# Eight pairs of the down projection's right half by seven products, with four small moves beside it

## The chip, the core and the metric

The kernel runs on one core of a Trainium2 chip. TensorE (PE in the profile) multiplies matrices into eight accumulator banks; VectorE (DVE), ScalarE (ACT) and GpSimd (POOL) do the elementwise work; SyncE (SP) and POOL issue the DMA transfers used here. The metric is the device time of one execution, in microseconds (us).

## The reference

Two layers, each a mixer (differential attention with eight heads beside a gated short convolution) and an MLP with squared ReLU, on 256 tokens of width 2048, all in float32:

```python
for l in range(DEPTH):
    h = _rmsnorm(x, attn_norm_g[l])
    proj = h @ w_in[l]
    ...
    x = x + jnp.concatenate([attn, conv.astype(attn.dtype)], axis=-1) @ w_out[l]

    hm = _rmsnorm(x, mlp_norm_g[l]) @ w_up[l]
    x = x + jnp.square(jax.nn.relu(hm)) @ w_down[l]
```

Here w_up is 2048 x 8192 and w_down 8192 x 2048, so the hidden activation of the MLP is 256 x 8192.

## The kernel before

Every product of float32 values is made of three matmuls. An operand is split into a high part (a copy to the float32r type on ScalarE) and a low part (value minus high part, on VectorE), and high x high, high x low and low x high are added up in an accumulator bank. So each weight tile costs one copy and one subtraction before TensorE can use it. TensorE's order is the program's own order, written out by hand. The other engines' instructions are ordered by a scheduler when the program is built, except those marked `late`, which keep their place.

Weights come as a list of jobs (`Weights`, line 283): a job loads a raw tile and splits it; `take` (line 353) hands out the next one and starts the jobs of the next three. There are three buffers for split halves. Small work beside the matmuls (transposes, attention, norms) is written as generators. `Background.tick` (line 74) is called between groups of matmuls; a generator that yields n goes on n ticks later.

The MLP (`mlp`, line 779) runs in two stages. The hidden activation is made in 32 pairs of 128 columns. While pair i comes out of the up projection (`up_part`, line 911), pair i - 2 goes into the left half of the down projection (columns 0 to 1023). Pairs 0 to 29 do this by seven products instead of eight: `square` (line 934) forms the sums S1 to S4 of the activation's quarters, `quarters` (line 818) forms sums of the weight's quarters (b1, b2, t13, t24), and `product` (line 958) is called seven times, with three matmuls of 512 columns each. Pairs 30 and 31 follow by ordinary products, 24 matmuls a pair (line 1042). The tile `h`, in which a pair's activation is formed, has one buffer. Each pair's squared activation is stored to DRAM (`hid`, line 943) from POOL's queue.

The second stage is the right half (columns 1024 to 2047, line 1069). It reads `hid` back in blocks of two pairs over SP's queue (`block`, line 1015), splits them again, and runs 16 blocks by two groups of 512 columns, all by ordinary products (`dn`, line 1081). Its pool opens only when the pool of the weight quarters has closed (line 1012). Then the next layer's norm begins: `norm.chunk` (line 439) transposes one quarter of x through two banks (`bank`, three buffers) and splits it.

In the mixer, `attention` (line 575) is started for each half of the heads three ticks after that half's v is done, and its last transposes come 12 ticks after its last unit. `Norm.factors` (line 484) broadcasts the ratio of the norm's two row factors with one small matmul (`rbc`, line 503), five ticks after the factors.

Of the kernel before, what the change touches and what calls it, by code (L numbers as in the profile page):

```python
# [15 lines left out]
P = 128  # L16
DEPTH = 2
D = 2048
S = 256
# [16 lines left out]
NB2 = DFF // (KG * P)  # L36

# [64 lines left out]
def trunk(ctx: ExitStack, tc: tile.TileContext, x, w_in, w_out, conv_w, q_norm_g, k_norm_g,  # L102
# [326 lines left out]
    class Norm:  # L429
# [54 lines left out]
        def factors(self):  # L484
# [8 lines left out]
            if self.which:  # L493
# [7 lines left out]
                yield 5  # L501
# [73 lines left out]
    def attention(l, qT, kT, kL, v, h0, dst, bias, tmp):  # L575
# [8 lines left out]
        def unit(i):  # L584
# [78 lines left out]
            yield 12  # L663
# [42 lines left out]
    def mixer(l, norm, loads):  # L706

        with ExitStack() as scope:
# [28 lines left out]
            for half in range(2):  # L737
# [15 lines left out]
                work.start(attention(l, qT, kT, kL, v, h0, cat[half], bias, tmp), 3)  # L753
# [25 lines left out]
    def mlp(l, mnorm, last):  # L779
# [3 lines left out]
        with ExitStack() as scope:  # L783
            upool = scope.enter_context(tc.tile_pool(name="upool", bufs=3))
            fpool = scope.enter_context(tc.tile_pool(name="fpool", bufs=2))
            dpool = scope.enter_context(tc.tile_pool(name="dpool", bufs=2))
            first = scope.enter_context(ExitStack())
            spool = first.enter_context(tc.tile_pool(name="spool", bufs=1))
# [22 lines left out]
            def load_rows(i, col):  # L811
                raw = dpool.tile([P, 2, 2 * CH], F32, tag="draw", name="draw")
# [5 lines left out]
            def quarters(i):  # L818


                keep = late if i == 0 else lambda ins: None
# [8 lines left out]
                def plain():  # L830
                    raw = forms["raw"] = load_rows(i, 0).rearrange("p k (n c) -> p k n c", n=2)
# [19 lines left out]
                if i == 0:  # L851
# [6 lines left out]
            def rows(i, k, box):  # L858
                def make():
                    if k == 0:  # L860
                        box.append(load_rows(i, 0))
# [22 lines left out]

            order = [(b - n, n) for b in range(NB2 + 1) for n in range(2) if 0 <= b - n < NB2]

# [12 lines left out]
            for b, n in order:  # L899
                box = []  # L900
                four(b, n, 0, box)
                four(b, n, 2, box)


            hid = [dram.tile([P, KG * S], F32, name=f"hid{l}{b}") for b in range(NB2)]
# [28 lines left out]
            def square(i, h):  # L934
# [8 lines left out]
                nc.gpsimd.dma_start(hid[i // 2][:, i % 2 * 2 * S:(i % 2 + 1) * 2 * S], u)  # L943
                n = 4
                if i < NP - LAG:
# [4 lines left out]
                    nc.vector.tensor_sub(h[:, S4], h[:, A12], h[:, S2])  # L950
                f = fpool.tile([P, 2, 8, P], F32R, tag="f", name="f")
# [6 lines left out]
            def product(n, j, a, b, stop=False):  # L958

                for m, (pa, pw) in enumerate(TERMS):  # L960
                    nc.tensor.matmul(prods[n], fs[j][:, pa, a], b[pw], start=(j == 0 and m == 0),  # L961
                                     stop=(stop and m == 2))

            fs = {}
            for i in range(NP):
# [14 lines left out]
                for c in range(2):  # L980
# [15 lines left out]
                    if j >= 0 and c == 0:  # L996
                        b11, b21, b22 = weights.take()
                        t1, t3 = weights.take()
                        product(1, j, A11, b11, end)
                        product(2, j, A12, b21)  # L1000
                        product(3, j, S4, b22)
                        product(5, j, S1, t1, end)
                        work.tick()
                    elif j >= 0:
                        t2, t4 = weights.take()
                        product(7, j, S3, t3, end)
                        product(6, j, S2, t2, end)
                        product(4, j, A22, t4)
                        work.tick()


            first.close()
            gpool = scope.enter_context(tc.tile_pool(name="gpool", bufs=3))

            def block(b):

                back = gpool.tile([P, KG * S], F32, tag="back", name="back", bufs=2)
                nc.sync.dma_start(back, hid[b])
                f = gpool.tile([P, 2, KG, S], F32R, tag="g", name="g")
                flat = f.rearrange("p a k s -> p a (k s)")  # L1020
                nc.scalar.activation(flat[:, 0], back, AF.Copy)
                nc.vector.tensor_sub(flat[:, 1], back, flat[:, 0].bitcast(F32))
                return f

            blocks = {0: block(0)}
# [5 lines left out]
            x11, x21, x12, x22 = (xs[n][:, t] for n in range(2) for t in range(NT))  # L1031
            e1, e2, e3, e4 = wide("e1"), wide("e2"), wide("e3"), wide("e4")
            nc.scalar.activation(e1, prods[1], AF.Copy, scale=mnorm.scale)
            onto(e2, prods[6], e1)
            onto(e4, prods[5], e2)
            onto(x22, prods[5], x22)
            onto(e3, prods[7], e2)
            for dst, v in ((x11, e1), (x12, e4), (x21, e3), (x22, e3)):
                nc.gpsimd.tensor_tensor(dst, dst, v, op=ALU.add)

            prods[8] = ps.tile([P, CH], F32, tag="av", name=f"pr{l}8", bufs=1)
            for j in range(NP - LAG, NP):
                for k in range(2):
                    b = weights.take()
                    for n, t, p in ((0, 0, 2), (0, 1, 4), (1, 0, 3), (1, 1, 8)):
                        for m, (pa, pw) in enumerate(TERMS):
                            nc.tensor.matmul(
                                prods[p], fs[j][:, pa, 2 * k + t], b[pw][:, n],
                                start=(p == 8 and j == NP - LAG and k == 0 and m == 0),
                                stop=(j == NP - 1 and k == 1 and m == 2))  # L1050
                    work.tick()
            for dst, p in ((x11, 2), (x21, 4), (x12, 3), (x22, 8)):
                onto(dst, prods[p], dst)
# [9 lines left out]
            else:  # L1063
# [77 lines left out]
```

## Time and profile before

| | |
|---|---|
| median of three runs | 2167.16 us |
| lowest and highest | 2166.77 and 2170.96 us |
| the profiled execution | 2167.59 us |
| its span, first to last instruction | 2165.8 us |
| mean granted TensorE clock | 0.999 |
| DMA, mean over the span | 206 GB/s |

How to read the lines below. A group's line names the source line, the engine, the operation, the output and inputs, their shapes and the count; then its busy time in us and the mean in ns; then the engine's idle time ahead of it and what ended that. A line of the chain is a start, a length and an instruction, for the sequence that ended last. In the table of waits the three numbers are the total in us, how often, and the longest. PEld is TensorE's weight load, which overlaps its matmuls.

### The profile page before, as it was taken

The numbers are of one execution on the slowest core, as the hardware profiler recorded it, in microseconds if no ns is written. First come the engines' busy times: TensorE is split into PE (matmuls) and PEld (weight loads), VectorE is DVE, ScalarE is ACT, GpSimd is POOL, SyncE is SP. The second block draws the span as 40 slices with busy tenths as digits, with TensorE's granted clock in tenths as the row PEclk, the third lists the DMA queues.
The fourth block names the chain that finished last, engine by engine and source line by source line (L and its number), as shares of the span: only waits on it lengthen the run. The fifth ranks groups of instructions, "written<-read, shape, count | busy, mean of one in ns | idle before, by whom it ended". The sixth has DMA issues, their size and how long they took to land.

```text
span 2165.8 us, 28903 instructions
## 1 busy us (share of the span) xinstructions
PE 2146.9 (99%) x10988; PEld 1828.7 (84%) x10988; DVE 1612.4 (74%) x2197; ACT 1294.1 (60%) x1743; POOL 135.3 (6%) x178
## 2 busy tenths in 40 slices
PE   9999999999999999999999999999999999999999
PEld 8888888888888888888888888888888888888887
DVE  6777655698888888855566776557988888887554
ACT  6666445566666666654456654446666666665443
POOL 3111100000000000100011111000000000001000
PEclk9999999999999999999999999999999999999999
DMA  8556666576666666577566566656766666666774
GB/s 271 179 162 210 189 188 186 170 235 216 214 211 214 218 216 215 196 257 242 174 213 176 160 215 190 185 165 204 233 211 213 216 219 215 211 213 211 246 242 147
DMA packets 292507, 446.62 MB, mean 206 GB/s; under 512 B 10419, under 2 KB 191237, under 8 KB 292368
## 3 DMA queue, kind: packets, MB, share of 16 engines
q1 hardware_dynamic: 285664, 423.66, 62.4%
q0 software_dynamic: 6656, 21.10, 2.5%
q8 instruction: 86, 1.41, 0.3%
q14 instruction: 53, 0.43, 0.1%
q10 hardware_dynamic: 48, 0.02, 0.0%
HBM read 425.84 MB, written 18.90 MB: 205 GB/s over the span
## 4 chain that ended last, share of the span: by engine, by line
PE 92%; DVE 3%; DMA 2%; ACT 2%; issue 1%; SPq 0%; DVEq 0%; ACTq 0%
PE upc L921 29%; PE dn L1081 16%; PE pr L961 13%; PE o L382 8%; PE gb L404 4%; PE k L382 4%; PE v L382 4%; PE ci L404 4%; PE q L382 4%; PE gc L404 3%; DMA raw<-in_w_in_dram 1%; PE upw L921 1%; PE sc L594 1%; DMA back<-hid 1%; DVE ulo L807 1%
## 5 line engine op out<-in xcount | busy, mean ns | idle before, releaser
L299 DVE TENSOR_TENSOR wlo<-raw,whi 128x1024 fp32r<-128x1024 f32 x382 | 468.9, 1229 | 364.1 <-ACT whi L298 363.3
L298 ACT ACTIVATE whi<-raw 128x1024 fp32r<-128x1024 f32 x382 | 404.6, 1060 | 448.9 <-PE dn L1081 167.8
L921 PE MATMUL upc<-nT,uhi 128*128 128x512 f32 x1920 | 477.5, 391 | 0.0
L806 ACT ACTIVATE uhi<-uraw 128x1024 fp32r<-128x1024 f32 x256 | 271.1, 1060 | 286.5 <-PE upc L921 253.4
L921 PEld LDWEIGHTS upc<-nT,uhi 128*128 128x128 f32 x1920 | 352.7, 188 | 68.2
L807 DVE TENSOR_TENSOR ulo<-uraw,uhi 128x1024 fp32r<-128x1024 f32 x256 | 312.8, 1222 | 113.5 <-ACT uhi L806 111.0
L1081 PE MATMUL dn<-whi,g 128*128 128x512 f32 x1024 | 316.3, 389 | 0.0
L921 PEld LDWEIGHTS upc<-nT,ulo 128*128 128x128 f32 x1920 | 261.9, 190 | 18.7
L921 PE MATMUL upc<-nT,ulo 128*128 128x256 f32 x1920 | 267.7, 282 | 0.0
L1081 PEld LDWEIGHTS dn<-whi,g 128*128 128x128 f32 x1024 | 192.2, 188 | 39.6
L1081 PE MATMUL dn<-wlo,g 128*128 128x512 f32 x512 | 199.7, 390 | 1.1 <-DVE wlo L299 0.9
L382 PE MATMUL o<-whi,cat 128*128 128x512 f32 x512 | 159.5, 390 | 0.0
L1081 PEld LDWEIGHTS dn<-wlo,g 128*128 128x128 f32 x512 | 96.1, 188 | 22.6 <-DVE wlo L299 2.8
L382 PEld LDWEIGHTS o<-whi,cat 128*128 128x128 f32 x512 | 96.2, 188 | 19.7
L382 PE MATMUL o<-wlo,cat 128*128 128x512 f32 x256 | 99.6, 389 | 0.0
L943 POOL DMA_DIRECT2D hid<-h x64 | 34.9, 545 | 946.0 <-ACT h L942 912.0
L961 PE MATMUL pr<-t13h,f 128*128 128x512 f32 x240 | 93.8, 391 | 0.0
L382 PE MATMUL k<-whi,nT 128*128 128x512 f32 x256 | 84.3, 396 | 0.0
L961 PE MATMUL pr<-t24h,f 128*128 128x512 f32 x240 | 84.0, 391 | 0.0
L961 PE MATMUL pr<-b2h,f 128*128 128x512 f32 x240 | 84.0, 391 | 0.0
L382 PE MATMUL v<-whi,nT 128*128 128x512 f32 x256 | 83.2, 395 | 0.0
L382 PE MATMUL q<-whi,nT 128*128 128x512 f32 x256 | 82.8, 394 | 0.0
(349 smaller groups left out, 3477.2 us busy)
## 6 DMA issues: line engine op xcount, KB each, us to landing
uraw<-in_w_up_dram SPq DMA_DIRECT2D x128, 1024.0 KB, 5.9
raw<-in_w_in_dram SPq DMA_DIRECT2D x191, 512.0 KB, 4.0
draw<-in_w_down_dram SPq DMA_DIRECT2D x64, 1024.0 KB, 5.1
raw<-in_w_down_dram SPq DMA_DIRECT2D x64, 1024.0 KB, 5.4
raw<-in_w_out_dram SPq DMA_DIRECT2D x64, 512.0 KB, 3.6
hid<-h POOLq DMA_DIRECT2D x64, 256.0 KB, 4.4
back<-hid SPq DMA_DIRECT2D x32, 512.0 KB, 3.4
rev<-by_dist_d POOLq DMA_DIRECT2D x4, 1024.0 KB, 10.0
```

The lines of the kernel that those rows point to most:

```text
L298: pair = (nc.scalar.activation(hi, raw, AF.Copy), nc.vector.tensor_sub(lo, raw, hi.bitcast(F32)))
L299: nc.vector.tensor_sub(lo, raw, hi.bitcast(F32)))
L382: nc.tensor.matmul(acc[:, t], a.ap[:, pa, k % KG, t * P:(t + 1) * P], (hi, lo)[pw][:, j], start=(k == 0 and n == 0), stop=(k == nk - 1 and ...
L404: nc.tensor.matmul(acc[:, f, 0] if part else acc[:, f], wt[:, k % 4, fs], a.ap[:, 0, k % KG] if part else a.ap[:, :, k % KG], start=(part ...
L594: nc.tensor.matmul(sc[m][:, OFF[t]:OFF[t] + W], qT[:, m, i, t * P:(t + 1) * P], k[:, m, i, :W], start=(k is kT), stop=(k is kL))
L806: nc.scalar.activation(hi, src, AF.Copy)
L807: nc.vector.tensor_sub(lo, src, hi.bitcast(F32))
L921: nc.tensor.matmul(acc[:, 0] if part else acc, wt[:, k], a.ap[:, 0, k % KG] if part else a.ap[:, :, k % KG], start=(part == 0 and kh == 0 ...
L943: nc.gpsimd.dma_start(hid[i // 2][:, i % 2 * 2 * S:(i % 2 + 1) * 2 * S], u)
L961: nc.tensor.matmul(prods[n], fs[j][:, pa, a], b[pw], start=(j == 0 and m == 0), stop=(stop and m == 2))
L1081: nc.tensor.matmul(acc[:, t], f[:, pa, k, t * P:(t + 1) * P], (hi, lo)[pw][:, k % 2], start=(b == 0 and k == 0 and m == 0), stop=(b == NB2 ...
```

## The change

- In the right half, pairs 2, 5, 8, 11, 14, 17, 20 and 23 go by seven products. The other pairs of 0 to 23 go by ordinary products, pair by pair; pairs 24 to 29 go in blocks as before. Pairs 30 and 31 are not stored and read back, but used first, from the tiles that the left half left in SBUF.
- A seven pair stores its activation with the sums (eight tiles of 128 columns instead of four), after the sums. Read-backs are issued from POOL's queue, into existing tiles, and their split goes to the pool that held the norm's transposed activation.
- The raw weight tiles of the MLP get a fourth buffer, and the lower quarters (b2) a second. The pool of the quarters stays open.
- The second half's attention starts six ticks after its v instead of three, and its last transposes come 18 ticks after the last unit instead of 12. The ratio's broadcast comes eight ticks after the factors instead of five.
- Chunks 0 and 1 of the next norm start 8 and 16 ticks after the right half's seven products are added to x (before: 12 and 24 ticks after the left half).

```diff
+SEVEN = (2, 5, 8, 11, 14, 17, 20, 23)
+BLK = 12
...
-                yield 5
+                yield 8
                 tp = bank("rbc")
...
-            yield 12
+            yield 12 if pace == 1 else 18
...
-                work.start(attention(l, qT, kT, kL, v, h0, cat[half], bias, tmp), 3)
+                work.start(attention(l, qT, kT, kL, v, h0, cat[half], bias, tmp,
+                                     1 + half), 3 * (1 + half))
...
-            upool = scope.enter_context(tc.tile_pool(name="upool", bufs=3))
+            upool = scope.enter_context(tc.tile_pool(name="upool", bufs=4))
...
-                    h2, l2 = parts(raw[:, 1], "b2", 1)
+                    h2, l2 = parts(raw[:, 1], "b2", 2)
...
-            order = [(b - n, n) for b in range(NB2 + 1) for n in range(2) if 0 <= b - n < NB2]
+            order = [(b - n, n) for b in range(BLK, NB2) for n in range(2)
+                     if BLK <= b - n < NB2 - 1]
...
+            blocks_of([(NB2 - 1, 0), (NB2 - 1, 1)])
+            for i in range(2 * BLK):
+                if i in SEVEN:
+                    weights.jobs += quarters(i, 2 * CH)
+                    continue
                 box = []
-                four(b, n, 0, box)
-                four(b, n, 2, box)
+                for k in range(2):
+                    rows(i, k, box, 2 * CH, upool, "uraw")
+            blocks_of(order)
...
-                nc.gpsimd.dma_start(hid[i // 2][:, i % 2 * 2 * S:(i % 2 + 1) * 2 * S], u)
+                if i not in SEVEN and i < NP - LAG:
+                    nc.gpsimd.dma_start(hid[i // 2][:, i % 2 * 2 * S:(i % 2 + 1) * 2 * S], u)
...
+                if i in SEVEN:
+                    nc.gpsimd.dma_start(hid7[i], h.rearrange("p a c -> p (a c)"))
...
+            def read_back(src, pool, tag, n):
+
+                back = (fpool.tile([P, 8, P], F32, tag="h", name="back", bufs=1) if n == 8 else
+                        nat.tile([P, 4, P], F32, tag="wide", name="back"))
+                nc.gpsimd.dma_start(back.rearrange("p a c -> p (a c)"), src)
+                f = pool.tile([P, 2, 8, P], F32R, tag=tag, name="fb")
+                nc.scalar.activation(f[:, 0, :n], back, AF.Copy)
+                nc.vector.tensor_sub(f[:, 1, :n], back, f[:, 0, :n].bitcast(F32))
+                return f
...
+            fs = {30: fs[30], 31: fs[31], 0: pair(0)}
+            for n in range(2):
+                columns(lambda k, pa, t: fs[NP - LAG + k // 2][:, pa, k % 2 * 2 + t], n, start=True)
+            for i in range(2 * BLK):
+                if i + 1 < 2 * BLK:
+                    fs[i + 1] = pair(i + 1)
+                else:
+                    blocks = {BLK: block(BLK)}
+                if i not in SEVEN:
+                    ordinary(fs[i])
+                    continue
...
+                for n, a, b in ((1, A11, b11), (2, A12, b21), (3, S4, b22), (5, S1, t1),
+                                (7, S3, t3), (6, S2, t2), (4, A22, t4)):
+                    own = n in (1, 5, 6, 7)
+                    product(n, fs[i], a, b, start and own, end and own)
+                    if n == 5:
+                        work.tick()
+                work.tick()
+            seven_onto(2, nc.vector)
+            if not last:
+                work.start(norm.chunk(0, 2), 8)
+                work.start(norm.chunk(1, 2), 16)
...
+            for b, n in order:
+                if n == 0 and b + 1 < NB2 - 1:
+                    blocks[b + 1] = block(b + 1)
+                columns(lambda k, pa, t, f=blocks[b]: f[:, pa, 2 * k + t], n,
+                        stop=(b == NB2 - 2))
```

`ordinary` and `columns` are the old loops of lines 1042 and 1076 made into functions; `seven_onto` is the old code of lines 1031 to 1039 (its additions to x on POOL for the left half, on VectorE for the right).

More of the change, by code (lines that the diff above doesn't have):

```diff
@@ L573, in qk_norm, with attention @@
             yield 1
-    def attention(l, qT, kT, kL, v, h0, dst, bias, tmp):
+    def attention(l, qT, kT, kL, v, h0, dst, bias, tmp, pace):
         parts = dst.open()
@@ L1062, in mlp, with columns @@
                 store(1)
-            else:
-                work.start(norm.chunk(0, 2), 12)
-                work.start(norm.chunk(1, 2), 24)
-            accs = {}
-            for b, n in order:
-                if n == 0:
-                    if b + 1 < NB2:
-                        blocks[b + 1] = block(b + 1)
-                if b == 0:
-                    accs[n] = mm.tile([P, NT, CH], F32, tag="mm2", name=f"dn{l}{n}")
-                f, acc = blocks[b], accs[n]
+            accs = [mm.tile([P, NT, CH], F32, tag="mm2", name=f"dn{l}{n}") for n in range(2)]
+            prods[2], prods[4] = accs[0][:, 0], accs[0][:, 1]
+            prods[3], prods[8] = accs[1][:, 0], accs[1][:, 1]
+            def columns(f, n, start=False, stop=False):
                 for kp in range(KG // 2):
```

123 lines of the change are left out of this document (68 added, 55 removed).

## Prediction

> **What bounds the kernel now.** I read the busy table of the page first, then the table of what TensorE waited for, then the chain of waits in order of time, then busy times by stage.
>
> ```profile
> PE 2146.9 (99%) x10988; PEld 1828.7 (84%) x10988; DVE 1612.4 (74%) x2197; ACT 1294.1 (60%) x1743; POOL 135.3 (6%) x178
> ```
> ```profile
> PE sc L594 <- ACT kT L545: 4.1, 2, 2.0
> PE pr L961 <- DVE f L953: 2.3, 3, 1.0
> PE atp L667 <- DVE an L658: 1.6, 2, 1.0
> PE pr L1047 <- DVE wlo L299: 1.6, 2, 0.8
> PE up L921 <- ACT ev L931: 1.4, 2, 0.7
> PE rbc L503 <- DVE diag L500: 1.1, 2, 0.5
> PE warm L156 <- DVE mhalf L148: 1.0, 1, 1.0
> PE dn L1081 <- DVE wlo L299: 0.9, 2, 0.5
> ```
> ```profile
> 165.62 2.79 PE gc L404 x16
> ...
> 604.03 5.56 PE upc L921 x32
> ...
> 948.66 130.58 PE dn L1081 x576
> ```
>
> TensorE is busy nearly everywhere, and its named waits sum to 14 us, each a fraction of a microsecond to 2 us. A matmul of 512 columns in the down projection takes 130.58/576 = 0.2267 us of the chain (its listed 0.39 us overlaps the next one). So the time is the number of matmuls, plus the waits. Every matmul taken away counts in full unless an engine that feeds TensorE falls behind.
>
> ```profile
> core 0: us, PE busy (x) PEld busy (x) DVE busy (x) ACT busy (x) POOL busy (x), PEclk, DMA share, GB/s
> ...
> 450.00:890.00 440.00, 438.70 (x2340) 378.62 (x2339) 389.71 (x525) 295.91 (x360) 15.14 (x28) 1.00 0.69 217
> ...
> 932.00:1089.00 157.00, 157.00 (x702) 130.25 (x701) 90.18 (x84) 77.11 (x85) 2.31 (x3) 1.00 0.64 208
> ```
>
> The first row is the up projection with the left half of the down projection by seven products: VectorE is busy 89% of TensorE's time, and TensorE hardly waits (2.3 us at L961 in both layers). The second is the right half, by ordinary products: VectorE at 57%. So the right half has VectorE time left, and seven products take VectorE time for fewer matmuls.
>
> **The change part by part.**
>
> *Matmuls.* A pair by ordinary products is 24 matmuls, by seven products 7 x 3 = 21. Eight pairs in each of two layers: 48 matmuls fewer, 48 x 0.2267 = **-10.9 us**. Nothing else changes the count.
>
> *Feeding the right half.* Three pairs (two ordinary, one by seven) are 69 matmuls, 15.64 us of TensorE.
>
> ```profile
> L299 DVE TENSOR_TENSOR wlo<-raw,whi 128x1024 fp32r<-128x1024 f32 x66 | 80.8, 1225 | 72.1 <-ACT whi L298 72.1
> ...
> L827 DVE TENSOR_TENSOR t13l<-t,t13h 128x1024 fp32r<-128x1024 f32 x28 | 34.3, 1226 | 0.8 <-ACT t13h L826 0.3
> L953 DVE TENSOR_TENSOR f<-h,f 128x1024 fp32r<-128x1024 f32 x28 | 34.2, 1220 | 0.0
> ...
> L827 DVE TENSOR_TENSOR b1l<-draw,b1h 128x512 fp32r<-128x512 f32 x27 | 18.5, 685 | 2.7 <-ACT b1h L826 2.7
> ...
> L953 DVE TENSOR_TENSOR f<-h,f 128x512 fp32r<-128x512 f32 x2 | 1.4, 722 | 0.0
> ```
>
> VectorE does for two ordinary pairs four low halves (4 x 1.225) and two 512-column read-back splits (2 x 0.722), 6.3 us; for a seven pair five operations of 128x1024 (b2, the first sums, t13, t24 and the read-back, 1.22 each) and three of 128x512 (b1 and two sums, 0.685 each), 8.2 us. Together 14.5 of 15.64 us, 93%. Successive rows of the timeline show that this overstates it:
>
> ```profile
> 902.79 2.56 POOL L1039 TENSOR_TENSOR x<-x,e 128x512 f32<-128x512 f32 x2
> ...
> 902.92 3.52 DVE L1022 TENSOR_TENSOR g<-back,g 128x1024 fp32r<-128x1024 f32 x1
> ...
> 906.37 1.21 DVE L299 TENSOR_TENSOR wlo<-draw,whi 128x1024 fp32r<-128x1024 f32 x1
> 907.50 1.21 DVE L1022 TENSOR_TENSOR g<-back,g 128x1024 fp32r<-128x1024 f32 x1
> 907.63 0.19 PEld L1047 LDWEIGHTS pr<-wlo,f 128*128 128x128 f32 x1 [1.21 <-DVE wlo L299]
> ```
>
> The operation that starts at 906.37 lists 1.21 us and the next starts 1.13 us later: back to back they overlap by 0.08 us. Fourteen of them give 13.4 us, 86%, which is less than the up stage carries already. In the changed program's order VectorE prepares a seven pair's quarters and sums during the two ordinary pairs ahead of it, so the 8.2 us need not fit into that pair's 4.8 us. Only the first two seven pairs are made in a heap behind the transition. I take **+1** for both layers; bounds 0 (as in the up stage) and 1.1 us, the whole margin of a group, lost twice a layer, +4.4. The read-backs go from SP's queue to POOL's, whose issues are near 0.54 us each; POOL has nothing else in this stage (2.31 us in the row above), and each read-back is issued a pair (5 us) or more ahead: 0, and if that cover went, VectorE's split is late, which is inside the bound.
>
> *Transition to the right half.* Before, the blocks read back could not load until the quarter tiles' pool closed, and their two splits stood on VectorE exactly when it also split the last weight rows; one took 3.52 us beside POOL's additions. TensorE waits 1.6 at L1047 and 0.9 at L1081. Afterwards the first 48 matmuls of the right half use pairs 30 and 31, still in SBUF, so no read-back is due for another 48 x 0.2267 = 10.9 us. POOL's four additions stay. **-2**; bounds -2.5 and 0.
>
> *Attention.* The second half's scores start three ticks later. Four ticks of the gate stage are the 16 matmuls that the chain gives 2.79 us, so three are 2.1 us, against a wait of 2.0 each. Its output transposes come six more ticks later, about 4.2 us against at most 1.0. Both waits go, 4.1 and 1.6. But VectorE has the same softmax to do, and TensorE now reaches its next transposes without the 2 us pause that covered for it: I let 1 us return. **-4.7**; bounds -5.7 and 0. Nothing later waits for this half: the output projection comes twelve column groups later.
>
> *Broadcast of the norm's ratio (yield 5 to 8).* The wait of 1.1 at rbc goes. In the changed order on VectorE, however, one 128x1024 weight split stands ahead of the last two splits of the last normalized chunk, where it stood behind them; the up projection needs that chunk next and gets it 1.1 us later. **0**; bounds -1.1 and +1.1.
>
> *Second buffer for the lower quarters.* In the up stage's first pairs it lets VectorE split the second pair's lower quarters ahead of the first pair's t13, where the single buffer made it stand behind. t13's low part is then one operation of 1.2 us later, at a place where TensorE waits now and then already (L961, 2.3 in all). **+2** for two layers; bounds 0 and +2.4.
>
> *Stores with sums.* A seven pair's store is 512 KB instead of 256 KB and is issued behind the last sum instead of behind the square; h has one buffer, so the next pair's first write waits for the landing.
>
> ```profile
> 602.74 0.54 POOL L943 DMA_DIRECT2D hid<-h  x1 [15.39 <-ACT h L942]
> ...
> 608.12 0.29 DVE L950 TENSOR_TENSOR h<-h 128x128 f32<-128x128 f32 x1
> ...
> 613.30 0.76 DVE L932 TENSOR_TENSOR h<-ev 128x256 f32<-128x256 f32 x2
> ```
> ```profile
> DMA to landing us min/median/max: 4.1/4.7/5.0
> ```
> ```profile
> draw<-in_w_down_dram SPq DMA_DIRECT2D x64, 1024.0 KB, 5.1
> ...
> back<-hid SPq DMA_DIRECT2D x32, 512.0 KB, 3.4
> ```
> ```profile
> DVE ulo L807 <- ACT uhi L806: 45.3, 52, 1.4
> ```
>
> In this timeline the last sum ends at 608.41 and the next write of h is at 613.30, 4.9 us on; in the changed order six operations (four of 1.14, two of 0.60 back to back) stand between, 5.8 us. The store lands in 4.7 now; 512 KB more costs 5.1 - 3.4 = 1.7 on SP's queue, so 256 KB more costs 0.85 and the landing is 5.5, an estimate from those rows. It just fits. If it is half a microsecond late 16 times, VectorE's own pauses in this stage (45.3 us over 28 pairs, 1.6 a pair) absorb it, except in the first pairs. **+1**; bounds 0 and +3. [...]
>
> *End of layer 0.* Counting ticks, chunk 1 of the next norm (16 + 2) and chunk 2 (two after the sixteenth) now come on the same tick: sixteen transposes in a row through three banks, where before they were apart (26 and later).
>
> ```profile
> L266 ACT ACTIVATE nT<-tpn,ngains 128x256 fp32r<-128x256 f32 x12 | 5.1, 468 | 2.9 <-DVE nT L267 2.9
> ```
> ```profile
> L267 DVE SCALAR_TENSOR_TENSOR nT<-tpn,ngains,nT 128x256 fp32r<-128x256 f32 x12 | 5.2, 479 | 0.5 <-ACT nT L266 0.5
> ```
>
> The fourth bank is free only when both halves of the first were read, by ScalarE and VectorE in turn: about four steps of 0.47, and up to one weight split of 1.2 ahead of them, 1.9 to 3.1. TensorE has 0.9 us of transposes meanwhile. **+2** once; bounds 0 and +3.1.
>
> *Sum.* -10.9 + 1 - 2 - 4.7 + 0 + 2 + 1 + 2 = -11.6. The profiled execution took 2167.59 (its span 2165.8 and 1.8 around it), 0.4 above the median of the runs, 2167.16. 2167.59 - 11.6 = **2156.0**.
>
> **The rivals.**
>
> *The waits only move.* The waits of attention and transition (4.7 and 2) come back at the next transposes or weight splits, since no engine but TensorE has less to do. For it: rbc's wait, which by the order of instructions moves to the last chunk. Against: at the transition two splits really fall away. Time 2156.0 + 6.7 = 2162.7. The matmuls stay saved.
>
> *VectorE becomes the bound in the right half: slower.* Suppose that the 14.5 us of listed durations are the true cost of a group, and that one operation in each meets work of POOL, which now has three read-backs to issue there, as the 3.52 row did, and loses the same 3.52 - 1.21 = 2.3 us. A group then takes VectorE 16.8 us, TensorE waits 16.8 - 15.64 = 1.2 in each of 16, 19 in all in place of the term of 1: 2156.0 + 18 = 2174. It decides from the point where a group costs VectorE more than 15.64 us. Against: the overlap in the timeline, and the up stage at 89% by the same count with POOL's stores in it.
>
> *The late store.* If twice the bytes take twice the landing, 9.4 us, h is free 9.4 - 5.8 = 3.6 us late in VectorE's queue, and the weight splits behind it wait too. One split pair feeds 16 matmuls, 5.56/2 = 2.78 us, and about one is in stock, so TensorE waits 0.8 a time: 16 x 0.8 = 13 in place of 1, 2168: the gain is gone. It decides from a landing of 5.8 + 2.8 = 8.6 us. Against: the two SP rows, where twice the bytes cost half as much again.
>
> **How the numbers follow.** Forecast 0.57, moved waits 0.22, VectorE 0.11, late store 0.10. The measurement can tell about 0.2%, 4.3 us: faster means below 2162.8, slower above 2171.5. The forecast's own range, by its bounds near the middle, is 2150 to 2162, all faster. Moved waits lie about that lower line: 0.13 faster, 0.09 same. VectorE's case ends above the upper line but for a tenth: 0.01 same, 0.10 slower. The late store lies below it, with its upper part beyond: 0.05 same, 0.05 slower. Faster 0.70, same 0.15, slower 0.15. With all terms at their best ends the sum is -10.9 - 2.5 - 5.7 - 1.1 = -20.2, 2147; at their worst -10.9 + 4.4 + 1.1 + 2.4 + 3 + 3.1 = +3.1, 2171. Leaving out a tenth on each side: 2150 to 2168.
>
> **What would show it.** The right half runs at 0.2267 us a matmul from its start, 744 matmuls in 169 us a layer; TensorE's waits name neither L594 nor L1047; VectorE is near 93% there by listed time. A wait of about 1 us stands at t13l of the first up pairs, one at the up projection's last chunk in place of rbc, one of about 2 us at the transposes at the end of layer 0. The seven pairs' stores land in 5 to 6 us. I am wrong if TensorE waits for low halves at many of the seven pairs, if stores land above 8 us, or if waits at the attention transposes add up to more than 3 us a layer.

## The result, and the profile after

| | before | after |
|---|---|---|
| median | 2166.97 us (2165.47 to 2170.96, 6 runs) | 2157.22 us (2154.73 to 2158.38, 6 runs) |
| ratio after to before | | 0.9948, 95% interval 0.9938 to 0.9958 |
| the profiled execution, its span | 2167.59 us, 2165.8 us | 2157.01 us, 2155.2 us |
| TensorE's named waits, all rows | 14.2 us | 14.1 us |

The kernel became 9.8 us faster by the medians, 10.6 by the profiled executions and 11.3 by the ratio. The kernel before was run again beside each group of experiments, with medians from 2167.8 to 2169.4. So I compare ratios to it, and turn a difference of ratios into time with 2167 us. Each ratio's interval is about 2 us to either side, so a difference of less than some 3 us between two kernels is read from their waits, not from their times.

The first line of the busy table of the kernel after:

```profile
PE 2136.4 (99%) x10940; PEld 1821.8 (85%) x10940; DVE 1696.0 (79%) x2315; ACT 1335.9 (62%) x1799; POOL 160.3 (7%) x228
```

TensorE issues 48 instructions fewer (10988 before), and its busy time falls by 10.5 us. VectorE has 84 us more to do. What TensorE waited for in the kernel after (total in us, times, longest):

```profile
PE pr L1059 <- DVE f L974: 3.0, 2, 1.5
PE atp L672 <- DVE mx L605: 3.0, 2, 1.5
PE tpn L451 <- DVE nT L271: 2.7, 1, 2.7
PE up L939 <- DVE nT L271: 1.5, 2, 0.7
PE up L939 <- ACT ev L949: 1.4, 2, 0.7
PE pr L982 <- DVE t13l L832: 1.2, 2, 0.6
PE warm L160 <- DVE mhalf L152: 1.0, 1, 1.0
PE upc L939 <- ACT ev L949: 0.3, 1, 0.3
```

Only the fifth and the seventh stood in the table before. The waits at the scores (4.1), at the second half's output transposes (1.6), at f L953 (2.3), at L1047 and L1081 (2.5) and at rbc (1.1) are gone. Waits at the split of pair 31 (L974), at the first half's output transposes (L672), at the norm's transposes (L451 and the first row of L939) and at t13l stand in their place, and the sum is the same. So by the waits the whole gain is the matmuls. Busy times in the up stage and in the part of the right half that has the seven pairs:

```profile
450.00:890.00 440.00, 439.71 (x2345) 379.68 (x2344) 391.12 (x524) 300.61 (x359) 14.60 (x27) 1.00 0.70 223
920.00:1035.00 115.00, 115.00 (x509) 95.20 (x509) 100.87 (x105) 73.18 (x82) 7.50 (x14) 1.00 0.72 246
```

In the second row TensorE is busy all of 115.00 us with 509 matmuls, 0.226 each, and VectorE is busy 100.87, 88%. Seven products run there without a pause.

### The profile page after: what moved, and what is told of

It reads as the page before. It is cut to its first block, busy times and chain, and to the rows that moved or that the text cites. A ratio compares the mean times of both kernels' runs of the same rounds, so it can differ in the third digit from the quotient of the medians.

```text
span 2155.2 us, 29063 instructions
## 1 busy us (share of the span) xinstructions
PE 2136.4 (99%) x10940; PEld 1821.8 (85%) x10940; DVE 1696.0 (79%) x2315; ACT 1335.9 (62%) x1799; POOL 160.3 (7%) x228
## 5 line engine op out<-in xcount | busy, mean ns | idle before, releaser
L303 DVE TENSOR_TENSOR wlo<-raw,whi 128x1024 fp32r<-128x1024 f32 x286 | 354.1, 1240 | 237.4 <-ACT whi L302 232.7
L302 ACT ACTIVATE whi<-raw 128x1024 fp32r<-128x1024 f32 x286 | 302.9, 1060 | 321.6 <-PE o L386 73.6
L939 PE MATMUL upc<-nT,uhi 128*128 128x512 f32 x1920 | 477.7, 391 | 0.3 <-ACT ev L949 0.3
L939 PEld LDWEIGHTS upc<-nT,uhi 128*128 128x128 f32 x1920 | 352.7, 188 | 68.9 <-ACT ev L949 0.7
L939 PEld LDWEIGHTS upc<-nT,ulo 128*128 128x128 f32 x1920 | 261.9, 190 | 18.7
L939 PE MATMUL upc<-nT,ulo 128*128 128x256 f32 x1920 | 267.7, 282 | 0.0
L1059 PE MATMUL dn<-whi,fb 128*128 128x512 f32 x512 | 160.3, 389 | 0.0
L1059 PEld LDWEIGHTS dn<-whi,fb 128*128 128x128 f32 x512 | 96.1, 188 | 20.1
L1059 PE MATMUL dn<-wlo,fb 128*128 128x512 f32 x256 | 99.6, 389 | 0.0
L832 DVE TENSOR_TENSOR t24l<-t,t24h 128x1024 fp32r<-128x1024 f32 x76 | 92.9, 1223 | 3.8 <-ACT t24h L831 1.4
L832 DVE TENSOR_TENSOR t13l<-t,t13h 128x1024 fp32r<-128x1024 f32 x76 | 92.8, 1221 | 3.5 <-ACT t13h L831 2.1
L832 DVE TENSOR_TENSOR b2l<-draw,b2h 128x1024 fp32r<-128x1024 f32 x76 | 92.4, 1216 | 0.8 <-ACT b2h L831 0.8
L845 DVE TENSOR_TENSOR t<-draw 128x1024 f32<-128x1024 f32 x76 | 92.5, 1217 | 0.0
L831 ACT ACTIVATE t24h<-t 128x1024 fp32r<-128x1024 f32 x76 | 79.9, 1051 | 8.3 <-PE dn L982 3.6
```

The costliest lines, as they stand in the source:

```text
L302: pair = (nc.scalar.activation(hi, raw, AF.Copy), nc.vector.tensor_sub(lo, raw, hi.bitcast(F32)))
L303: nc.vector.tensor_sub(lo, raw, hi.bitcast(F32)))
L831: keep(nc.scalar.activation(hi, src, AF.Copy))
L832: keep(nc.vector.tensor_sub(lo, src, hi.bitcast(F32)))
L845: keep(nc.vector.tensor_sub(t[:, 0:2], raw[:, :, 1], raw[:, 0]))
L939: nc.tensor.matmul(acc[:, 0] if part else acc, wt[:, k], a.ap[:, 0, k % KG] if part else a.ap[:, :, k % KG], start=(part == 0 and kh == 0 ...
```

## The experiments

Each is an edit to the changed kernel, but for one that edits the kernel before. Line numbers are those of each profile.

**Is the gain the matmuls?** No pair of the right half by seven products; with them go their longer stores and the additions that end them, and all else is kept:

```diff
-SEVEN = (2, 5, 8, 11, 14, 17, 20, 23)
+SEVEN = ()
```

> Edit to the changed kernel: no pair of the right half is made by seven products (all 24 ordinary); everything else of the change stays. Theory A (the whole gain is the 48 matmuls, the moved traces only trade one wait for another): TensorE issues 48 more matmuls at 0.227 us, so 2157.2 + 10.9 = about 2168, as before within 2 us, and the waits of attention, of the up stage's start and of the transition stay as in the changed kernel. Rival B (the prediction's own terms for the moved traces hold: attention -4.7, transition -2, against +2 for the second buffer and +2 at layer 0's end): 2167 - 2.7 = about 2164. Rival C (feeding seven products costs VectorE time that TensorE waits for, the prediction's +1 and the 11 in 100 of a VectorE bound): less than 10.9 comes back, 2164 to 2166, and the right half's waits get fewer than they are now.

Measured: 2169.24 us beside 2169.22 of the kernel before, ratio 0.9999 (0.9990 to 1.0007). From 0.9948 that is 11.1 us, the 10.9 of theory A. B, some 3 us below the kernel before, lies outside the interval. C's upper end does not; it falls because the right half's seven products have no row in the table of waits of the kernel after, so there is no wait to get fewer. The new structure, with every moved trace in it, is worth nothing in sum, within 2 us.

**What are the later traces worth?** Undone in the changed kernel (`yield 18` to 12, `3 * (1 + half)` to 3, `yield 8` to 5):

> Edit to the changed kernel: the second half's attention starts after 3 ticks again, its last pause is 12 ticks again, and the broadcast of the factors waits 5 ticks again; the seven products stay. The prediction's terms (attention -4.7, broadcast 0): undone, 2157.2 + 4.7 = about 2162; the waits at the scores (about 2.2 us a layer) and at the second half's output transposes come back and nothing goes. Theory A (a wait for a wait): the scores' wait of 2.2 us a layer comes back, and the 1.6 us a layer at the first half's output transposes goes, as does 0.5 in the up stage: +1 to +2, about 2158.5. Rival C (the moved traces cost time): 2156 or less.

Measured: 2159.71 us, ratio 0.9958 (0.9945 to 0.9972), 2.2 us slower than with them. The two intervals overlap, so the waits have to carry the reading. The first two rows of the table of waits:

```profile
PE sc L599 <- ACT kT L549: 4.1, 2, 2.0
PE gc L408 <- ACT whi L302: 3.2, 2, 1.7
```

The scores' wait is back and L672 is gone, as theory A said. But the rows that it names (the scores, rbc, L672 and the up stage) change the sum by 0.7 us only. The second row, a wait for a weight's high part, is in no theory and not in the kernel before, and its cause is not shown. All rows of the table add up to 17.7 us, 3.6 more than in the kernel after; 1.3 come off for the half clock below, which this run did not show (granted clock 1.00 behind its pause). So the size is theory A's, and its account is incomplete. And the same traces put alone into the kernel before:

```diff
-            yield 12
+            yield 12 if h0 == 0 else 18
-                work.start(attention(l, qT, kT, kL, v, h0, cat[half], bias, tmp), 3)
+                work.start(attention(l, qT, kT, kL, v, h0, cat[half], bias, tmp), 3 * (1 + half))
-                yield 5
+                yield 8
```

> Edit to the kernel before: only the later traces are put in (second half of the attention after 6 ticks, last pause of 18, broadcast after 8 ticks), no seven products in the right half. The prediction's terms: -4.7, 2162.5. Theory A (from the run in which they were undone: 2 to 2.5 us): ratio 0.9985 to 0.9995, 2165 to 2166, the scores' wait of 2.2 us a layer replaced by 1.6 at the first half's output transposes. Rival C (they bring nothing without the rest of the change): 2167 to 2168.

Measured: 2166.67 us, ratio 0.9988 (0.9979 to 0.9996), -2.6 us. The ratio is within theory A's, and C's "nothing" and the prediction's -4.7 lie just outside the interval. The first row of its table of waits is the one that takes the scores' place:

```profile
PE atp L667 <- DVE mx L600: 3.0, 2, 1.5
```

**What is this new wait?** The second half's scores, now started at 161.1 us, fall between the first half's two groups of output transposes. The second group needs a third PSUM bank, and the scores hold two of the three until VectorE has added the bias. With the groups 4 ticks apart:

```diff
-                yield 2
+                yield 4 if pace == 1 else 2
```

> Edit to the changed kernel: in the first half's attention the second group of output transposes follows 4 ticks after the first instead of 2. Theory A (the 1.65 us a layer there is the wait for a third PSUM bank, which the second half's scores, now between the two groups, hold until VectorE has added the bias at 164.0): two ticks are 1 to 2 us, the wait goes or falls under 0.5 a layer, 2157.2 - 2.5 = about 2154.5. Rival K (VectorE is what is late, at whatever tick the transposes stand, and the scores' successors then wait): the 1.65 comes back at the next transposes or the next scores, 2157.

Measured: 2154.36 us, ratio 0.9937 (0.9925 to 0.9950), -2.4 us; no row of L672 is left in the table of waits. Theory A: the wait does not come back elsewhere, as rival K had it. That a bank is what was waited for is read from the program and from the row's VectorE operation, the one that reads the scores' banks.

**The split of pair 31.** VectorE and GpSimd at the transition, timeline of the kernel after (start, length, instruction):

```profile
899.82 0.73 DVE L1036 SCALAR_TENSOR_TENSOR e<-pr,rowf,e 128x512 f32<-128x512 f32 x1
899.89 3.77 POOL L1050 TENSOR_TENSOR x<-x,e 128x512 f32<-128x512 f32 x3
900.48 3.75 DVE L974 TENSOR_TENSOR f<-h,f 128x512 fp32r<-128x512 f32 x1
...
904.28 0.50 PE L1059 MATMUL pr<-whi,f 128*128 128x512 f32 x1 [1.52 <-DVE f L974]
```

The split starts 0.59 us after the first of GpSimd's three additions and ends 0.57 us after the last. Three of the four additions moved behind VectorE's:

```diff
-                for dst, v in ((x11, e1), (x12, e4), (x21, e3), (x22, e3)):
+                adds = ((x11, e1), (x12, e4), (x21, e3), (x22, e3))
+                for dst, v in (adds if n else adds[:1]):
                     engine.tensor_tensor(dst, dst, v, op=ALU.add)
+                return adds[1:]
...
                     onto(xs[n][:, t], prods[((2, 4), (3, 8))[n][t]], xs[n][:, t])
+            for dst, v in adds:
+                nc.gpsimd.tensor_tensor(dst, dst, v, op=ALU.add)
```

> Edit to the changed kernel: where the left half's seven products are added to the residual, GpSimd does the first of its four additions at once, and the other three only after VectorE has added the last four products; the result is the same. Theory E (VectorE's split of pair 31, 3.75 us at 900.48 for a shape that takes 0.75 elsewhere, is held up by the three GpSimd additions at 899.89 to 903.66, and TensorE's 1.7 us a layer at L1059 is all due to that): the split takes 0.75 us, the wait goes, 2157.2 - 3.4 = about 2154, unless the additions hold up a VectorE operation for which TensorE waits later. Rival F (the split is late because ScalarE's squares are late or VectorE is full): the split stays over 2 us or the wait stays over 1 us a layer, 2157. [...]

Measured: 2156.34 us, ratio 0.9942 (0.9930 to 0.9955), -1.3 us, too little for the intervals to tell. Its timeline and its table of waits:

```profile
900.54 0.68 DVE L974 TENSOR_TENSOR f<-h,f 128x512 fp32r<-128x512 f32 x1
...
908.20 4.90 POOL L1075 TENSOR_TENSOR x<-x,e 128x512 f32<-128x512 f32 x3 [3.55 <-DVE x L1036]
910.01 1.95 DVE L303 TENSOR_TENSOR wlo<-raw,whi 128x1024 fp32r<-128x1024 f32 x1
911.88 2.31 DVE L1084 TENSOR_TENSOR fb<-back,fb 128x1024 fp32r<-128x1024 f32 x1
```
```profile
PE dn L1116 <- DVE wlo L303: 1.8, 2, 0.9
```

The split takes 0.68 us at the same place in VectorE's order, so the additions were its cause (E). The 3.0 us at L1059 are gone, and 1.8 came at the lower weights, because two later VectorE operations, beside the moved additions (908.20 to 913.10), now list 1.95 and 2.31 for 1.22: the exception that E names. Net -1.2 by the waits.

**The second buffer for the lower quarters**, taken back:

```diff
-                    h2, l2 = parts(raw[:, 1], "b2", 2)
+                    h2, l2 = parts(raw[:, 1], "b2", 1)
```

> Edit to the changed kernel: the lower quarters have one buffer again instead of two; all else stays. The prediction's term (the second buffer costs 2 us by a late t13l in the up stage's first pairs): 2157.2 - 2 = about 2155, the 0.8 us a layer at t13l gone. Theory A (the second buffer pays for itself: it took away the waits at b1h, 1.2 to 1.6 us a layer in the kernel before, for 0.8 at t13l): about 2159 to 2161, a wait of 1 to 3 us a layer at b1h near the first pairs. Rival D (the right half's seven products need the second buffer, since ordinary pairs lie between them): each of the 16 waits 0.3 us or more, 2163 or more.

Measured: 2164.85 us, ratio 0.9979 (0.9970 to 0.9988), 6.7 us slower. The prediction's sign was wrong and theory A's size too small; rival D's place (the right half) is wrong as well. Two rows of its table of waits, and VectorE with ScalarE in its timeline:

```profile
PE pr L982 <- ACT f L973: 3.3, 2, 1.6
...
PE pr L982 <- DVE f L974: 2.8, 2, 1.5
```
```profile
461.44 0.63 ACT L831 ACTIVATE b1h<-draw 128x512 fp32r<-128x512 f32 x1 [2.53 <-DMA draw<-in_w_down_dram]
...
462.10 0.69 DVE L832 TENSOR_TENSOR b1l<-draw,b1h 128x512 fp32r<-128x512 f32 x1
462.71 0.76 DVE L950 TENSOR_TENSOR h<-ev 128x256 f32<-128x256 f32 x2
```

With one buffer VectorE's order has the write of `h` behind a b1l, and that waits for ScalarE and a load. In the kernel after the same write stands 7 us earlier:

```profile
455.49 0.75 DVE L950 TENSOR_TENSOR h<-ev 128x256 f32<-128x256 f32 x2
```

So the activation of that pair is late, once a layer. That this order follows from the one buffer is read from the timeline; I did not try the order alone.

**The stores.** In the kernel after, the table of landing times of the 16 stores with sums, and VectorE's waits for them:

```profile
DMA to landing us min/median/max: 3.0/6.9/8.3
```
```profile
DVE h L950 <- DMA hid1s<-h: 11.4, 6, 2.7
...
DVE h L950 <- DMA hid0s<-h: 8.8, 6, 2.4
```

VectorE waits 20.2 us in all, and no row of TensorE names the activation of a stored pair. How far does the cover reach? Each such store issued twice:

```diff
                 if i in SEVEN:
+                    nc.gpsimd.dma_start(hid7x[i], h.rearrange("p a c -> p (a c)"))
                     nc.gpsimd.dma_start(hid7[i], h.rearrange("p a c -> p (a c)"))
```

> Edit to the changed kernel: each of the 16 pairs that go by seven products in the right half stores its eight tiles twice, first to a scratch tensor and then where they are read back. The stores of 512 KB land 6.5 to 7.6 us after issue now, where the prediction had 5.5; the rival of the late store has TensorE wait from 8.6 us on. With a second 512 KB ahead the landing should be 9 to 10.5 us. Theory O (VectorE's next write of the stored tile waits for the landing, 9 to 11 us a layer already, but TensorE is covered by products of the pair before): under 3 us more, 2157 to 2160. Rival P (the cover ends near 8.6 us, and then each us of the landing is one of TensorE): 16 stores lose 1 to 2 us each, 2170 to 2185, with waits named f in the up stage.

Measured: 2168.50 us, ratio 1.0001 (0.9992 to 1.0009), 11.5 us slower: between O and P by time. Landing of the second store, who waited for it, and TensorE's new waits:

```profile
  DVE h L952: 64.7, 16
...
DMA to landing us min/median/max: 8.7/9.6/10.6
```
```profile
PE pr L985 <- ACT f L976: 3.7, 2, 1.9
...
PE pr L985 <- DVE f L977: 2.0, 2, 1.0
```

VectorE waits at all 16 stores, 4 us each, but TensorE waits for an activation only behind the first store of each layer (near 474 and 1552 us), where VectorE works without a pause (462.4 to 476.9 in layer 0): 5.7 us in the two layers together, each followed by some 3 us of matmuls at half clock (a granted clock of 0.50 in layer 0; last section), about 3 us more. That is 9 of the 11.5; the rest I did not find. At the others the cover holds beyond 8.6 us.

**The end of layer 0.** Chunk 1 of the next norm started at 13 ticks:

```diff
-                work.start(norm.chunk(1, 2), 16)
+                work.start(norm.chunk(1, 2), 13)
```

> Edit to the changed kernel: at the end of layer 0 the second chunk's normalization starts 13 ticks after the right half instead of 16, so that the transposes of the two chunks no longer fall on one tick. The prediction puts +2 us on that place. The trace of the changed kernel shows 2.7 us of waiting at the transposes there and then nine matmuls at 0.43 us instead of 0.227 at a granted clock of 0.50, together some 4.2 us. Theory H (the half clock follows from the pause): both go, 2157.2 - 4 = about 2153. Rival I (the half clock comes from elsewhere): only the wait goes, 2154.5, and the matmuls at 0.43 stay. Rival J (the wait moves to the chunk's own vector work, its sums of squares or its factor): 2156 to 2157.

Measured: 2152.88 us, ratio 0.9931 (0.9919 to 0.9944), -3.7 us. TensorE there in the timeline of the kernel after, then busy times with the granted clock (third figure from the end), after first, then with 13 ticks:

```profile
1070.78 1.47 PE L451 MATMUL tpn<-ident,x 128*128 128x128 f32 x12
1074.92 1.09 PE L451 MATMUL tpn<-ident,x 128*128 128x128 f32 x4 [2.67 <-DVE nT L271]
...
1076.23 0.63 PE L1112 MATMUL dn<-wlo,fb 128*128 128x512 f32 x1
1076.66 1.05 PE L1112 MATMUL dn<-whi,fb 128*128 128x512 f32 x2
```
```profile
1075.60:1078.00 2.40, 2.40 (x8) 1.92 (x8) 0.00 (x0) 0.00 (x0) 0.00 (x0) 0.50 0.00 0
1078.00:1082.00 4.00, 4.00 (x19) 3.33 (x18) 1.27 (x3) 2.22 (x5) 0.00 (x0) 1.00 0.00 0
```
```profile
1075.60:1078.00 2.40, 2.40 (x12) 1.97 (x12) 0.97 (x3) 1.92 (x4) 1.21 (x2) 1.00 0.00 0
```

Twelve transposes, a pause of 2.67 us, four more, and then matmuls 0.43 us apart (1076.23 to 1076.66) at a granted clock of 0.50. The 2.4 us of that row do the work of 1.2, and the four transposes ahead ran slow too (0.50 from 1074.92 to 1075.60), so the clock costs about 1.3 us on top of the pause. With 13 ticks the pause and the half clock are both gone (1.00): theory H.

**Where does VectorE become the bound?** Twelve pairs, every second one, by seven products:

```diff
-SEVEN = (2, 5, 8, 11, 14, 17, 20, 23)
+SEVEN = (1, 3, 5, 7, 9, 11, 13, 15, 17, 19, 21, 23)
```

> Edit to the changed kernel: 12 of the right half's 24 pairs, every second one, go by seven products instead of 8, every third. 24 matmuls fewer are 5.4 us. In a group of one ordinary and one seven pair TensorE has 45 matmuls, 10.2 us; VectorE has 11.3 us by listed times (two weights of 1.22 and a split of 0.69 against 0.69 + 1.22 + 1.22 + 0.69 + 0.69 + 1.22 + 1.22 + 1.22), and 10.4 us when each starts 0.083 us before the one ahead of it ends, as the trace shows. Theory L (VectorE limits, by back-to-back times): 24 groups lose 0.2 us, 2157.2 - 5.4 + 5 = about 2157. Rival M (by listed times, or waits for loads and ScalarE add to it): +26 - 5.4, about 2178. Rival N (buffers cover it): 2152.

Measured: 2195.11 us, ratio 1.0128 (1.0112 to 1.0143): 39 us slower than with eight, more than theory M. TensorE waits 21.1 us for the t24 parts (the two rows below, 20.4, and 0.7 at t24h). All named waits grow by 29 us; with the 5.4 us of matmuls saved, some 15 us of the loss stand in no row (a stretch of 3.4 us at a granted clock of 0.57, in the last section, is part of them). In the right half VectorE is busy only 119.06 of 135 us:

```profile
PE pr0r L982 <- DVE t24l L832: 12.8, 9, 2.4
PE pr1r L982 <- DVE t24l L832: 7.6, 8, 2.2
```
```profile
925.00:1060.00 135.00, 121.74 (x514) 96.41 (x513) 119.06 (x125) 79.28 (x91) 8.56 (x16) 0.99 0.64 227
```
```profile
ACT b1h L831 <- DMA draw<-in_w_down_dram: 31.5, 8, 6.7
...
SPq L818 <- DVE t L849: 71.5, 10, 10.3
```

So VectorE alone does not explain it. The last two rows (same window) show a loop: the load of the next quarters waits until VectorE's last sum has freed one of two raw buffers, and ScalarE and then VectorE wait for that load (ScalarE 31.5 us here, 0.4 in the kernel after). A third raw buffer for the quarters, for which the other weights gave up their fourth:

```diff
-            upool = scope.enter_context(tc.tile_pool(name="upool", bufs=4))
+            upool = scope.enter_context(tc.tile_pool(name="upool", bufs=3))
-            dpool = scope.enter_context(tc.tile_pool(name="dpool", bufs=2))
+            dpool = scope.enter_context(tc.tile_pool(name="dpool", bufs=3))
```

> Edit to the kernel with 12 pairs by seven products: the raw rows of the quarters get a third buffer, and the raw tiles of the other weights three buffers instead of four, to make room. In the kernel with 12 TensorE waits 21 us at the t24 parts, while VectorE's listed share is 88%, and the load of the next quarters waits until VectorE's last sum has freed one of the two raw buffers. Theory S (the loop of load, split, sum is what limits it): with a third buffer the waits at t24 fall below 6 us, about 2195 - 20 = 2175, less what the fourth buffer of the other weights was worth. Theory T (VectorE's own work limits it): they stay above 15 us, 2188 to 2197.

Measured: 2170.20 us, ratio 1.0009 (1.0000 to 1.0019), 26 us less. The waits for the t24 parts of the right half fall to 8.4 us, and in the same window:

```profile
925.00:1060.00 135.00, 130.80 (x572) 106.83 (x571) 130.32 (x139) 88.78 (x103) 10.87 (x19) 1.00 0.72 248
```

Theory S by time, though the waits stay above the 6 us that it gave; ScalarE's wait for the load of the quarters has no row any more. VectorE is now busy 97%, and with its work at that mark twelve pairs, with one weight buffer less, are still 13 us slower than eight. Not all of that is the right half: 3.0 us are a wait for the activation at the start of the up stage (f L974), which the kernel with eight does not have.

**The mends together.** 13 ticks and 4 ticks; and the same with the later additions:

> The same without the moved additions: 13 ticks and 4 ticks apart. Theory Q: 2157.2 - 4.3 - 2.9 = about 2150, and the 1.7 us a layer at L1059 stays; against it the run with all three shows what the moved additions bring by themselves, 1.2 us by the trace (1.7 a layer gone, 1.1 a layer come at the lower weights) and nothing if the new wait is the same work later.

> The changed kernel with three of the edits above together: the second chunk's normalization starts after 13 ticks, the first half's output transposes lie 4 ticks apart, and three of GpSimd's four additions follow after the last four products. If the three places are independent (theory Q), their measured gains add up: 4.3 + 2.9 + 0.9, 2157.2 - 8 = about 2149, ratio to the kernel before 0.9910 to 0.9920. If they share VectorE time or one pause takes over from another (rival R), 2151 to 2153.

Measured: two 2150.27 us, ratio 0.9915 (0.9902 to 0.9929); three 2150.19 us, ratio 0.9912 (0.9899 to 0.9926). Theory Q, near 2149. Both beat the changed kernel, by 7 to 8 us, and the interval with all three does not touch its 0.9938. The later additions by themselves cannot be told from nothing. All that TensorE waits for with the three:

```profile
PE dn L1116 <- DVE wlo L303: 1.8, 2, 0.9
PE up L939 <- DVE nT L271: 1.5, 2, 0.7
PE up L939 <- ACT ev L949: 1.4, 2, 0.7
PE pr L982 <- DVE t13l L832: 1.2, 2, 0.6
PE warm L160 <- DVE mhalf L152: 1.0, 1, 1.0
PE upc L939 <- ACT ev L949: 0.2, 1, 0.2
```

That is 7.1 us, against 14.1 without the mends.

## Why the prediction came out

The time, 2157.2 against a forecast of 2156.0, came out. The matmuls, the broadcast and, within its bounds, the feeding of the right half were right. Attention and transition were booked too high as gains, the second buffer had the wrong sign, the end of layer 0 was too small. Beside the matmuls the terms summed to -0.7 and came to about +1, because these errors cancelled: that part is luck.

| term | predicted | measured | from |
|---|---|---|---|
| matmuls | -10.9 | -11.1 | the run without seven pairs |
| feeding the right half | +1 | 0 | waits after: no row there |
| transition | -2 | +0.5 | 2.5 of waits gone, 3.0 come |
| attention and broadcast | -4.7 + 0 | -2.2 | traces undone |
| second lower-quarter buffer | +2 | -1.3 | 2.5 of waits gone (f L953, t24l), 1.2 come |
| stores with sums | +1 | 0 | waits after |
| end of layer 0 | +2 | +4 | 2.7 of wait, 1.3 of half clock |
| sum | -11.6 | -10 | -9.8 by the medians |

- **Matmuls**: right, and the only term that carries the result.
- **Feeding**: right. Between 920 and 1035 us VectorE's listed durations sum to 108.8 us of 115, 95%, for the 93% of the prediction; without their overlaps it is busy 88%, for its 86%. No seven pair waits. The rival with VectorE as the bound fell for eight pairs. With twelve VectorE ends at 97% and the gain is lost, though a load ring of two buffers costs more first, which the prediction's count of VectorE time did not see.
- **Transition**: the two named waits did go. The step that failed is "POOL's four additions stay", costed at nothing. The row of 3.52 us, for an operation of 1.21, showed what they do to VectorE beside them; before, that operation was a read-back's split, and TensorE waited 0.8 us a layer for the weight split right behind it (L1047). With that split gone, the one beside the additions is pair 31's, which TensorE needs next.
- **Attention**: both waits went, as said. What failed is "I let 1 us return", with the place given only as the next transposes. The 3.0 us came at the first half's transposes, which the change does not move, through the PSUM banks. The edit of their distance showed it.
- **Broadcast**: right in kind and size. rbc's 1.1 became 1.5 at the up projection's first pair, for the last chunk's splits.
- **Second buffer**: the wait at t13l came (1.2), as the order of instructions said. What failed is that this was the whole account: the step left out what the single buffer held up, though f L953 stood in the table of waits with 2.3. In the changed kernel the second buffer is worth 6.7.
- **Stores**: the landing was mis-sized, 6.9 for 5.5. The estimate took differences of medians on another queue; here a store of the same 512 KB lands in 3.0 to 8.3. The slowest passed the 8 us that the prediction named as a sign of being wrong, and still cost TensorE nothing: the absorption by VectorE's pauses, on which the term rested, held. The rival of the late store was wrong in its threshold: 9.6 us costs TensorE once a layer, not at 16 stores.
- **End of layer 0**: place and cause right. The wait was within its bounds (2.7 for up to 3.1); the 1.3 us of half clock behind it had no part in the sum.
- **The rival that the waits only move** was right about the waits: 14.2 became 14.1. It gave 2162.7 because it kept the prediction's +6 of new waits beside it. By the table, the gains of 6.7 that I hoped for came to 1.7, and the losses of 6 to 2.7.

Not tried: VectorE's order with a single lower-quarter buffer, all additions on VectorE, and the fourth raw weight buffer by itself.

## What to carry to other kernels

TensorE was busy 99% here, and the 48 matmuls taken from it counted in full (11.1 us measured for 10.9), but the waits that were shifted came back in other places (14.2 us before, 14.1 after), one of them, by the program, at a shared PSUM bank. So list every user of the bank or tile between the old place and the new one before a gain is booked. When a second buffer is costed, ask what the single one holds up now, and read that from the table of waits. When more work goes to a feeding engine, follow its load ring too: with every second pair the ring of two raw buffers cost at least 26 us before VectorE was full.

## What the hardware showed that I had not expected

**A pause can be paid twice.** Of eight kernels here with the pause of 2.7 us at the end of layer 0, six ran the matmuls behind it at half clock for some 3 us. The granted clock was 0.50 over 3.1 us in the kernel after; 0.57 over 4 us without seven pairs and with one lower-quarter buffer, 0.58 with 4 ticks, 0.64 with the later additions; 0.54 and 0.61 in two stretches of 2 us with twelve pairs and the third raw buffer. Two did not: it was 1.00 with the traces undone and in the first kernel with twelve pairs. Pauses of 1.9 and 1.0 us with two matmuls between them, in the kernel with doubled stores, were followed by it too, in both layers (in layer 1 the granted clock was 0.72 from 1552.8 to 1556.0 us and 0.80 in the 4 us after; layer 0 is this row):

```profile
475.60:478.80 3.20, 3.13 (x7) 2.51 (x8) 2.32 (x6) 1.72 (x3) 0.00 (x0) 0.50 0.68 184
```

With one lower-quarter buffer, two pauses in the same place (1.6 and 1.5 us in layer 0, 1.6 and 1.3 in layer 1) were followed by it in layer 1 only (0.52 from 1552.8 to 1556.0 us, against 1.00 from 475.6 to 478.8 in layer 0). In the first kernel with twelve pairs a pause of 2.41 us was (0.57 from 970.6 to 974.0). In the kernels before and after none of the eleven single pauses of 1.0 to 2.04 us was: the granted clock is 1.00 in the 3 us behind each. Why it comes behind some pauses of one length and not behind others, these runs do not show. The 2.7 us lie between transposes; what these add to it is not separated here.

**GpSimd's additions held a VectorE operation up.** The split of 0.68 us took 3.75 beside three additions (3.77 together) and ended 0.57 after the last of them; in layer 1 it took 3.74. With the additions moved it took 0.68 in the same place. Beside the moved ones, which took 4.90, two operations of 1.22 took 1.95 and 2.31. What makes the one engine wait for the other, these traces do not show.

**Stores landed later where the DMA engines were busier.** The 512 KB stores of the kernel after landed in 3.0 to 8.3 us. The first kernel with twelve pairs has stores of the same size, of other pairs, and most land in 2.9:

```profile
DMA to landing us min/median/max: 2.9/2.9/7.5
```

They divide by how busy the DMA engines are in the 3 us behind the issue. Two rows for such windows, the kernel after and the one with twelve (the DMA share is the last figure but one); the first store landed in 7.0 us, the second in 2.9:

```profile
585.02:588.02 3.00, 3.00 (x15) 2.49 (x14) 3.00 (x5) 2.01 (x3) 0.54 (x1) 1.00 0.88 203
...
564.37:567.37 3.00, 3.00 (x17) 2.57 (x16) 2.16 (x2) 3.00 (x4) 0.54 (x1) 1.00 0.64 262
```

Of the 40 stores of the two kernels, the 22 with a share up to 0.69 landed in 2.9 to 4.3 us, and the 18 with 0.79 or more in 3.7 to 8.3. In the kernel after alone, the two with a share of 0.63 and 0.68 landed in 3.1 and 3.0, and the 14 others in 3.7 to 8.3.
